# Seven block products in place of eight for two pairs of chunks of the second feed-forward

## The chip, the cores and the metric

The kernel runs on one core of a Trainium2 chip. A core has TensorE (PE; its weight loads are PEld), VectorE (DVE), ScalarE (ACT), GpSimd (POOL), SyncE (SP), whose queue issues most transfers, and 16 DMA engines. The on-chip memory SBUF has 128 partitions; matmul results go to banks of 128 x 512 fp32 in PSUM. The metric is the device time of one execution in microseconds. The median of three runs before is 800.43 us.

## What is computed

One residual block on x (256 tokens of 1024 values): a feed-forward, a mixer of two branches, a read of a memory by attention, and a second feed-forward. The change touches the last:

```python
def swiglu(h, w_in, w_down):
    gate, up = jnp.split(h @ w_in, 2, axis=-1)
    return (jax.nn.silu(gate) * up) @ w_down

h = rmsnorm(x, ffn2_pre_g[l])
x = x + 0.5 * rmsnorm(swiglu(h, ffn2_w_in[l], ffn2_w_down[l]), ffn2_post_g[l])
```

`w_in` is 1024 x 5632 (2816 gate and 2816 up columns), `w_down` 2816 x 1024.

## The kernel before

**Numbers.** Each fp32 operand of a large product is split into two fp32r parts, hi (a cast on ACT) and lo = operand − hi (a subtraction on DVE). A product is three matmuls: hi·hi, hi·lo, lo·hi. A weight "unit" is 128 x 1024 fp32, 512 KB: `load_split` (L118 to L128) loads it into one of 4 `raw` buffers over SP's queue, casts it into one of 8 `hi` buffers (L126) and subtracts into one of 8 `lo` buffers (L127). The same eight and eight serve all weights in turn.

**The feed-forward** (`ffn`). The inner width is cut into 11 chunks of 256 (NFF). A chunk's 512 columns (256 gate, 256 up) are four units; unit i holds the rows of two blocks kb = 2i and 2i + 1 of 128 each, side by side. `act_tok(c, h)` computes chunk c for token half h (128 tokens) in one PSUM bank (tag `mm`, two banks): 8 blocks x 3 = 24 matmuls of 128 x 128 by 128 x 512, the tokens transposed and stationary (`X.hi`, `X.lo`), the weights moving. `act_evac` applies silu on ACT (L354) and the product with the up half on DVE (L359); both scale by `r2[h]`, the per-token factor of the norm, so that TensorE works on unscaled tokens. `flush` transposes a finished chunk (four transposes, L349) and splits it into `acts`. `down(c, h)` is the second product: 2 units of `w_down`, 12 matmuls for each half, added up over all chunks in four banks of tag `acc`.

**Order.** In the second feed-forward chunks 0 and 1 run first for half 0, then for half 1 (the tokens of half 1 come later, from the block before). From chunk 2 on each step is `act_tok(c, 0)`, `act_tok(c, 1)`, `down(c − 2)` with a flush. The last three second products run at the end, half by half, with `post` and `post_last`. The framework places each instruction on its engine by readiness and program order; `after` ties a group behind a given matmul. Each engine takes its own instructions in the order that results, and a transfer waits in SP's queue until its buffer is free.

**Buffers.** Tag `m4` has 21 buffers of 4 KB in a partition, for tokens, activations, gain rows and whatever else is 128 x 1024. Tag `extra` has 4 of 4 KB: four of the eight `heads` loaded at the start (L460) and the four rows of gate biases (L829) use it. `row_of` (L244 to L253) turns the two per-token factors, one for each partition, into a row along the free axis on all partitions: two products of a diagonal matrix with ones, then a copy by ACT. GpSimd does next to nothing: some memsets, a few transfers, two selects, and one sum in `post_last` (L328) beside two DVE operations (L330).

Of the kernel before, what the change touches and what calls it, by code (L numbers as in the profile page):

```python
# [9 lines left out]
F32 = mybir.dt.float32  # L10
# [36 lines left out]
WARM = 8  # L47

X_AT = 11


_ORDER = [
# [15 lines left out]
def block_kernel(ctx: ExitStack, tc: tile.TileContext, wts, head_in, gf_in, x_in, mem_in, memT_in, cols, rows, fbias, masks, out):  # L68
# [12 lines left out]
    def MM(*args, **kw):  # L81
        log.append(PE.matmul(*args, **kw).ins)  # L82
# [9 lines left out]
    def nm(s):  # L92
        count[0] += 1
        return f"{s}_{count[0]}"

    def m4(shape, dt=F32, n="m"):
        return mp.tile(shape, dt, tag="m4", name=nm(n))
# [7 lines left out]
    def mm():  # L105
        return pp.tile([P, 512], F32, tag="mm", name=nm("mm"), bufs=2)

    def trp():
        return pp.tile([P, 512], F32, tag="tr", name=nm("tr"), bufs=2)
# [5 lines left out]
    def parts_of():  # L115
        return [wp.tile([P, D], F32R, tag=t, name=nm(t), bufs=8) for t in ("hi", "lo")]
# [27 lines left out]
    def split(hi, lo, src):  # L144
        S.copy(hi, src)  # L145
        V.tensor_tensor(out=lo, in0=src, in1=hi.bitcast(F32), op=ALU.subtract)
# [43 lines left out]
    def bc(a, shape, dim):  # L190
        return a.unsqueeze(dim).to_broadcast(shape)
# [52 lines left out]
    def row_of(r2):  # L244

        ps = trp()
        for h in range(2):
            dg = sp.tile([P, P], F32, tag="diag", name=nm("diag"), bufs=2)
            V.tensor_scalar(out=dg, in0=ident, scalar1=r2[h], scalar2=None, op0=ALU.mult)
            MM(ps[:, h * P : (h + 1) * P], ones, dg, start=True, stop=True)  # L250
        row = sp.tile([P, T], F32, tag="row", name=nm("row"), bufs=2)
        S.copy(row, ps[:, :T])
        return row  # L253

    def gain_split(X, kb, src, g, a=0, b=T, first=False):
# [4 lines left out]
            S.activation(X.hi(kb, a, b), src, AF.Copy, scale=gs)  # L260
        V.scalar_tensor_tensor(out=X.lo(kb, a, b), in0=src, scalar=gs, in1=X.hi(kb, a, b).bitcast(F32), op0=ALU.mult, op1=ALU.subtract)  # L261

    def to_T(X, src, h, g, qs=(0, 1)):

        for q in qs:
            ps = trp()
            for j in range(4):
                kb = 4 * q + j
                PE.transpose(ps[:, j * P : (j + 1) * P], src(kb), ident)  # L269
            for j in range(4):  # L270
                gain_split(X, 4 * q + j, ps[:, j * P : (j + 1) * P], g, h * P, h * P + P)
# [62 lines left out]
    def ffn(w_in, w_dn, X, r2, n_tok, i_row, first_half, second_half=None):  # L334

        acts = {}
        late = []
        ats = {}

        def flush(n):  # L340

            if late:
                c = late.pop(0)
                tr = trp()
                trv = tr.rearrange("p (j t) -> p j t", j=2)
                with after(n):
                    for h in range(2):
                        for j in range(2):
                            PE.transpose(trv[:, j, h * P : (h + 1) * P], ats[c, h][:, j * P : (j + 1) * P], ident)  # L349
                    split(acts[c][:, 0], acts[c][:, 1], trv)  # L350

        def act_evac(ps, c, h):
            sg = sp.tile([P, FC], F32, tag="c1", name=nm("sg"), bufs=7)
            silu = S.activation(sg, ps[:, :FC], AF.Silu, scale=r2[h])  # L354
            if c == NFF - 1 and h == 1 and not first_half:
                with tc.issue_after(silu.ins):
                    S.activation(warm, ones[:, 0:1], AF.Sqrt)
            a = sp.tile([P, FC], F32, tag="c1", name=nm("at"), bufs=7)
            V.scalar_tensor_tensor(out=a, in0=ps[:, FC:], scalar=r2[h], in1=sg, op0=ALU.mult, op1=ALU.mult)  # L359
            ats[c, h] = a  # L360
            if h == 1:
                late.append(c)

        def act_tok(c, h):
            ps = mm()
            proj_tok(ps, X, chunk(w_in, c), h)
            act_evac(ps, c, h)

        def act_first(c, bank):

            u = chunk(w_in, c)
            outs = [bank(), bank()]
            for kb in range(KB):
                wh, wl = blk(u, kb)
                for i in range(3):
                    for h in range(2):
                        a, b = h * P, h * P + P
                        x, w = ((X.hi(kb, a, b), wh), (X.lo(kb, a, b), wh), (X.hi(kb, a, b), wl))[i]
                        MM(outs[h], x, w, start=(kb == 0 and i == 0), stop=(kb == KB - 1 and i == 2))
            return outs  # L380

        def down(c, h, cols=((0, 512), (512, 1024))):
            act = acts[c]
            hs = slice(h * P, (h + 1) * P)
            for j in range(2):
                wh, wl = unit(w_dn, 2 * c + j)
                ah, al = act[:, 0, j, hs], act[:, 1, j, hs]
                for lo, up in cols:
                    for i, (a, w) in enumerate(((ah, wh), (ah, wl), (al, wh))):
                        MM(accs[h][lo // 512][:, lo % 512 : lo % 512 + up - lo], a, w[:, lo:up], start=(c == 0 and j == 0 and i == 0), stop=(c == NFF - 1 and j == 1 and i == 2))  # L390

        for c in range(n_tok):
            acts[c] = m4([P, 2, 2, T], F32R, "act")
        for h in range(2):
            m = len(log)
            for c in range(n_tok):
                act_tok(c, h)
            if h == 0 and n_tok:
                second_half(m)
        accs = None  # L400
        done = 0
        if callable(r2):
            outs = [act_first(c, acc) for c in range(2)]
            r2 = r2()
            for c in range(2):
                acts[c] = m4([P, 2, 2, T], F32R, "act")
                for h in range(2):
                    act_evac(outs[c][h], c, h)
            n_tok = 2
        for c in range(n_tok, NFF):  # L410
            acts[c] = m4([P, 2, 2, T], F32R, "act")
            if c == 2 and first_half:
                n = len(log)
                outs = act_first(c, mm)
                for h in range(2):
                    flush(n + L_ACT + 24 * h)
                    act_evac(outs[h], c, h)
            else:
                for h in range(2):
                    n = len(log)  # L420
                    act_tok(c, h)
                    if c == 2 or c > NFF - STAG + 1:
                        flush(n + L_ACT)
            if c == 6:
                grow = load_row(i_row)
                if first_half:
                    with tc.issue_after(loads[-1]):
                        nc.sync.dma_start(masks_s, masks)
            if accs is None:
                accs = [[acc(), acc()], [acc(), acc()]]  # L430
            while done < min(c - 1, NFF - STAG):
                n = len(log)
                for h in range(2):
                    down(done, h)
                flush(n + L_ACT)
                done += 1
        left, right = (0, 512), (512, 1024)
        m = len(log)
        for cut in (left, right):
            for c in range(NFF - STAG, NFF):  # L440
                down(c, 0, (cut,))
        flush(m + L_ACT)
        post(accs[0], 0, grow, 0.5, not first_half)
        m = len(log)
        if first_half:
            for c in range(NFF - STAG, NFF):
                down(c, 1)
            first_half(m)
            post(accs[1], 1, grow, 0.5)
        else:  # L450
            for cut in (left, right):
                for c in range(NFF - STAG, NFF):
                    down(c, 1, (cut,))
            post_last(accs[1], 1, grow, 0.5)
# [2 lines left out]


    X1 = Pair()
    heads = [wp.tile([P, D], F32, tag="raw" if kb < 4 else "extra", name=nm("head"), bufs=4) for kb in range(KB)]  # L460
    for kb in range(KB):
        loads.append(nc.sync.dma_start(heads[kb][:, : T + 512 + KB], head_in[kb]).ins)

# [358 lines left out]


    zs = []

    def gates(c):
        u = chunk("gates", c)
        z = m4([P, 2, 512], n="zg")
        brow = wp.tile([P, D], F32, tag="extra", name=nm("brow"), bufs=4)[:, :512]  # L829
        with tc.issue_after(loads[-1]):  # L830
            nc.sync.dma_start(brow, rows[4 + c // 2, c % 2 * 512 : c % 2 * 512 + 512].partition_broadcast(P))
        for h in range(2):
            ps = mm()
            proj_tok(ps, X2, u, h)
            V.scalar_tensor_tensor(out=z[:, h], in0=ps, scalar=r2[h], in1=brow, op0=ALU.mult, op1=ALU.add)
        zs.append(z)
# [268 lines left out]
```

## Time and profile before

| | us |
|---|---|
| median of three runs (lowest, highest) | 800.43 (800.04, 800.54) |
| span of the profiled execution, first to last instruction | 798.5 |
| mean granted TensorE clock in it | 0.999 |
| ACT busy in the span | 418.6 |
| second feed-forward from chunk 3 to the end of chunk 9 | 645.87 to 763.50 |
| span from 776.18 to the end (last second products and norm) | 22.32 |

The profile gives the profiled execution by its span; what lies before the first and after the last instruction is in the time of the runs only. In lines of groups the columns are line, engine, operation, out<-in with shapes, count, then busy us and the mean ns of one, then the idle time of the engine ahead of them and what ended it. In the chain of waits each line has its start, its length and the work. In windows each engine's busy time stands with the number of its instructions behind it; the last three numbers are the granted clock, the DMA share and GB/s.

### The profile page before, as it was taken

The numbers are of one execution on the slowest core, as the hardware profiler recorded it, in microseconds if no ns is written. First come the engines' busy times: TensorE is split into PE (matmuls) and PEld (weight loads), VectorE is DVE, ScalarE is ACT, GpSimd is POOL, SyncE is SP. The second block draws the span as 40 slices with busy tenths as digits, with TensorE's granted clock in tenths as the row PEclk, the third lists the DMA queues.
The fourth block names the chain that finished last, engine by engine and source line by source line (L and its number), as shares of the span: only waits on it lengthen the run. The fifth ranks groups of instructions, "written<-read, shape, count | busy, mean of one in ns | idle before, by whom it ended". The sixth has DMA issues, their size and how long they took to land.

```text
span 798.5 us, 12835 instructions
## 1 busy us (share of the span) xinstructions
PE 789.4 (99%) x5068; PEld 682.3 (85%) x5068; DVE 520.4 (65%) x824; ACT 418.6 (52%) x636; POOL 9.2 (1%) x21
## 2 busy tenths in 40 slices
PE   9999999999999999999999999999999999999996
PEld 7888888888899999998888888999888888888885
DVE  6765545548766898578675765965649754545543
ACT  7655345446853447348574445655647654434541
POOL 0000000000000100100000000000000000000000
PEclk9999999999999999999999999999999999999999
DMA  9775654664545555744476655556443666664521
GB/s 348 244 262 210 219 181 161 198 219 149 170 160 142 179 188 161 237 146 140 156 272 236 199 173 166 159 185 203 143 145 131 212 190 215 205 203 163 181 83 53
DMA packets 43692, 147.45 MB, mean 185 GB/s; under 512 B 4840, under 2 KB 8304, under 8 KB 43632
## 3 DMA queue, kind: packets, MB, share of 16 engines
q1 hardware_dynamic: 43024, 144.92, 54.7%
q0 software_dynamic: 464, 1.58, 0.7%
q8 instruction: 40, 0.66, 0.3%
q14 instruction: 20, 0.16, 0.1%
q10 hardware_dynamic: 144, 0.13, 0.0%
HBM read 145.56 MB, written 1.06 MB: 184 GB/s over the span
## 4 chain that ended last, share of the span: by engine, by line
PE 98%; DMA 0%; DVE 0%; issue 0%; ACT 0%; DVEq 0%; ACTq 0%
PE mm L82 67%; PE acc L82 27%; PE tr L349 1%; PE tr L82 1%; PE tr L269 1%; DMA head<-in_head_dram 0%; PE tr L785 0%; PE tr L871 0%; PE tr L974 0%; DVEq L1101 0%; DVE xs L330 0%; DVE post L315 0%; ACT hi L475 0%; ACT hT L145 0%; ACT junk L232 0%
## 5 line engine op out<-in xcount | busy, mean ns | idle before, releaser
L127 DVE TENSOR_TENSOR lo<-raw,hi 128x1024 fp32r<-128x1024 f32 (+1 forms) x260 | 311.3, 1206 | 124.7 <-ACT hi L126 115.7
L126 ACT CAST hi<-raw 128x1024 fp32r<-128x1024 f32 (+1 forms) x260 | 266.4, 1038 | 156.2 <-PE mm L82 95.2
L82 PE MATMUL mm<-hi,hT 128*128 128x512 f32 (+1 forms) x592 | 227.0, 386 | 0.0
L82 PE MATMUL mm<-lo,hT 128*128 128x512 f32 (+1 forms) x592 | 227.0, 386 | 0.0
L82 PE MATMUL mm<-hi,lT 128*128 128x512 f32 (+1 forms) x592 | 226.3, 386 | 0.0
L82 PEld LDWEIGHTS mm<-hi,hT 128*128 128x128 f32 x592 | 111.1, 188 | 21.9 <-ACT hT L260 0.5
L82 PEld LDWEIGHTS mm<-hi,lT 128*128 128x128 f32 x592 | 111.1, 188 | 21.8 <-DVE lT L261 0.5
L82 PEld LDWEIGHTS mm<-lo,hT 128*128 128x128 f32 x592 | 111.0, 188 | 20.6
L82 PE MATMUL acc<-hi,act 128*128 128x512 f32 x352 | 111.9, 390 | 0.0
L82 PE MATMUL mm<-hT,hi 128*128 128x256 f32 x384 | 109.0, 284 | 0.1
L82 PE MATMUL mm<-hT,lo 128*128 128x256 f32 x384 | 109.0, 284 | 0.0
L82 PE MATMUL mm<-lT,hi 128*128 128x256 f32 x384 | 108.9, 284 | 0.0
L82 PEld LDWEIGHTS acc<-hi,act 128*128 128x128 f32 x352 | 66.1, 188 | 13.2
L82 PEld LDWEIGHTS mm<-hT,hi 128*128 128x128 f32 x384 | 73.6, 192 | 0.4 <-issue 0.3
L82 PEld LDWEIGHTS mm<-hT,lo 128*128 128x128 f32 x384 | 73.6, 192 | 0.1
L82 PEld LDWEIGHTS mm<-lT,hi 128*128 128x128 f32 x384 | 73.6, 192 | 0.1
L82 PE MATMUL acc<-lo,act 128*128 128x512 f32 x176 | 70.0, 398 | 0.0
L354 ACT ACTIVATE sg<-mm,rstd 128x256 f32<-128x256 f32 x40 | 19.0, 475 | 75.0 <-PE mm L82 75.0
L359 DVE SCALAR_TENSOR_TENSOR at<-mm,rstd,sg 128x256 f32<-128x256 f32 x40 | 19.2, 481 | 57.1 <-ACT sg L354 57.1
L82 PEld LDWEIGHTS acc<-lo,act 128*128 128x128 f32 x176 | 33.1, 188 | 6.2
L82 PE MATMUL acc<-hi,hT 128*128 128x512 f32 x96 | 35.3, 395 | 0.2
L82 PE MATMUL acc<-hi,lT 128*128 128x512 f32 x96 | 35.3, 395 | 0.0
(194 smaller groups left out, 644.9 us busy)
## 6 DMA issues: line engine op xcount, KB each, us to landing
raw<-in_wts_dram SPq DMA_DIRECT2D x248, 512.0 KB, 4.5
raw<-in_gf_dram SPq DMA_DIRECT2D x12, 344.0 KB, 3.9
head<-in_head_dram SPq DMA_DIRECT2D x8, 388.0 KB, 6.1
grow<-in_rows_dram SPq DMA_DIRECT2D x4, 512.0 KB, 5.5
xs<-in_x_dram SPq DMA_DIRECT2D x2, 512.0 KB, 8.6
cbm<-cd POOLq DMA_DIRECT2D x2, 512.0 KB, 7.0
brow<-in_rows_dram SPq DMA_DIRECT2D x4, 256.0 KB, 5.5
memT<-in_memT_dram SPq DMA_DIRECT2D x2, 512.0 KB, 6.8
```

Source lines behind the costliest of these rows:

```text
L82: log.append(PE.matmul(*args, **kw).ins)
L126: S.copy(h, r)
L127: V.tensor_tensor(out=l, in0=r, in1=h.bitcast(F32), op=ALU.subtract)
L269: PE.transpose(ps[:, j * P : (j + 1) * P], src(kb), ident)
L349: PE.transpose(trv[:, j, h * P : (h + 1) * P], ats[c, h][:, j * P : (j + 1) * P], ident)
L354: silu = S.activation(sg, ps[:, :FC], AF.Silu, scale=r2[h])
L359: V.scalar_tensor_tensor(out=a, in0=ps[:, FC:], scalar=r2[h], in1=sg, op0=ALU.mult, op1=ALU.mult)
```

## The change

Chunks 4 and 5, and chunks 7 and 8, are computed together (a "quad", `QUADS = (4, 7)`). The tokens are cut in two halves h, the 1024 rows of the weights into even and odd blocks j, the columns into the two chunks. That makes a 2 x 2 by 2 x 2 product of blocks, each block product 4 row blocks x 3 = 12 matmuls. Winograd's form of Strassen's scheme computes it with 7 block products: X00·B11, X01·B21, S1·T1, S2·T2, S3·T3, X11·T4, S4·B22. S1 to S4 are sums of token blocks, T1 to T4 sums of weight blocks.

Since tokens of the two halves are now added, the per-token factor must be in them: `mixed`, called once after chunk 2, adds hi and lo of the tokens, multiplies by the row of factors, and splits again (GpSimd, then ACT and DVE); it forms and splits S1 to S4. From chunk 3 on all chunks use the scaled tokens, and `act_evac` has no scale.

In `quad` the units of the first chunk go to `raw`, those of the second to two buffers `wide` of two units each. GpSimd forms A = B11 + B12 and E = B21 + B22 unit by unit, then T2 = A + B22, T3 = B12 + B22 and T4 = A + E, in the order of the code; T1 is A. `two` splits each sum. B12 itself is never split, and B11, B21 and B22 are. Partial results are copied out of PSUM by ACT (`keep`) and combined on DVE. The second products `down(n_down, ...)` of the two chunks that are due stand between the block products, half by half. No flush stands inside a quad; chunk 6 and chunk 9 flush after each half instead.

`heads` 4 to 7 and the gate-bias rows use halves of `wide` in place of `extra`.

```diff
+QUADS = (4, 7)
+    def mixed(X, r):
+        row = row_of(r)
+        full = [m4([P, 4, T], n="full") for _ in range(2)]
+        for f, xh, xl in zip(full, X.h, X.l):
+            G.tensor_tensor(out=f, in0=xh.bitcast(F32), in1=xl.bitcast(F32), op=ALU.add)
+            G.tensor_tensor(out=f, in0=f, in1=bc(row, [P, 4, T], 1), op=ALU.mult)
+        N = Pair()
+        for q in range(2):
+            split(N.h[q], N.l[q], full[q])
+        sums = [m4([P, 2, 4, P], n="sums") for _ in range(2)]
+        s1_, s2_, s3_, s4_ = (t[:, i] for t in sums for i in range(2))
+        def form(o, x, y, op):
+            for q in range(2):
+                G.tensor_tensor(out=o[:, 2 * q : 2 * q + 2], in0=x(q), in1=y(q), op=op)
...
+        form(s1_, block(1, 0), block(1, 1), ALU.subtract)
+        form(s2_, of(s1_), block(0, 0), ALU.subtract)
+        form(s3_, block(0, 0), block(1, 0), ALU.subtract)
+        form(s4_, block(0, 1), of(s2_), ALU.add)
+        out = []
+        for t in sums:
+            hi, lo = m4([P, 2, 4, P], F32R, "sh"), m4([P, 2, 4, P], F32R, "sl")
+            split(hi, lo, t)
+            out += [(hi[:, i], lo[:, i]) for i in range(2)]
+        return N, out
...
         def act_evac(ps, c, h):
             sg = sp.tile([P, FC], F32, tag="c1", name=nm("sg"), bufs=7)
-            silu = S.activation(sg, ps[:, :FC], AF.Silu, scale=r2[h])
+            if mix:
+                silu = S.activation(sg, ps[:, :FC], AF.Silu)
+            else:
+                silu = S.activation(sg, ps[:, :FC], AF.Silu, scale=r2[h])
...
-            if h == 1:
+            if (c, 1 - h) in ats:
                 late.append(c)
+        def quad(c, n_down):
+            N, ((s1h, s1l), (s2h, s2l), (s3h, s3l), (s4h, s4l)) = mix[0]
+            for k in (c, c + 1):
+                acts[k] = m4([P, 2, 2, T], F32R, "act")
+            def two(src):
+                hi, lo = (p.rearrange("p (i n) -> p i n", i=2) for p in parts_of())
+                split(hi, lo, src)
+                return [(hi[:, i], lo[:, i]) for i in range(2)]
+            B11, B21, T1, wide, ones_, sums = [], [], [], [], [], []
+            for q in range(2):
+                W = wp.tile([P, 2, 2, 512], F32, tag="wide", name=nm("wide"), bufs=2)
+                A, E = m4([P, 2, 512], n="ta"), m4([P, 2, 512], n="te")
+                for i in range(2):
+                    u = _AT[w_in] + 4 * c + 2 * q + i
+                    raw = wp.tile([P, D], F32, tag="raw", name=nm("raw"), bufs=4)
+                    loads.append(nc.sync.dma_start(raw, wts[u - 4]).ins)
+                    loads.append(nc.sync.dma_start(W[:, i].rearrange("p j n -> p (j n)"), wts[u]).ins)
+                    hi, lo = parts_of()
+                    split(hi, lo, raw)
+                    B11.append((hi[:, :512], lo[:, :512]))
+                    B21.append((hi[:, 512:], lo[:, 512:]))
+                    G.tensor_tensor(out=A[:, i], in0=raw[:, :512], in1=W[:, i, 0], op=ALU.add)
+                    G.tensor_tensor(out=E[:, i], in0=raw[:, 512:], in1=W[:, i, 1], op=ALU.add)
+                wide.append(W)
+                ones_.append((A, E))
+            for A, E in ones_:
+                T1 += two(A)
...
+            b1, b2, b3 = mm(), mm(), trp()
+            for i in range(4):
+                prod(b1, X(0, 0), B11, i, True)
+                prod(b3, X(0, 1), B21, i, True, True)
+            p1 = keep(b1)
+            prods(b2, F(s1h, s1l), T1, True)
+            V.tensor_tensor(out=p1, in0=p1, in1=b3, op=ALU.add)
+            act_evac(p1, c, 0)
+            T2 = []
+            for (A, E), W in zip(ones_, wide):
+                t = m4([P, 2, 512], n="t2")
+                G.tensor_tensor(out=t, in0=A, in1=W[:, :, 1], op=ALU.add)
+                T2 += two(t)
+            down(n_down, 0)
+            prods(b1, F(s2h, s2l), T2, False)
+            w = keep(b1)
+            T3 = []
+            for W in wide:
+                t = m4([P, 2, 512], n="t3")
+                G.tensor_tensor(out=t, in0=W[:, :, 0], in1=W[:, :, 1], op=ALU.add)
+                T3 += two(t)
+            down(n_down, 1)
+            prods(b1, F(s3h, s3l), T3, False)
+            v = keep(b1)
+            V.tensor_tensor(out=v, in0=b2, in1=v, op=ALU.subtract)
+            act_evac(v, c + 1, 1)
+            T4 = []
+            for A, E in ones_:
+                G.tensor_tensor(out=E, in0=A, in1=E, op=ALU.add)
+                T4 += two(E)
+            down(n_down + 1, 0)
+            prods(b1, X(1, 1), T4, False, True)
+            act_evac(b1, c, 1)
+            B22 = []
+            for W in wide:
+                B22 += two(W[:, :, 1])
+            down(n_down + 1, 1)
+            prods(b2, F(s4h, s4l), B22, False, True)
+            V.tensor_tensor(out=w, in0=b2, in1=w, op=ALU.subtract)
+            act_evac(w, c + 1, 0)
...
+            if not first_half and c in QUADS:
+                quad(c, done)
+                done += 2
+                continue
...
-                    if c == 2 or c > NFF - STAG + 1:
+                    if c == 2 or c > NFF - STAG + 1 or c - 2 in QUADS and not first_half:
                         flush(n + L_ACT)
+            if c == QUADS[0] - 2 and not first_half:
+                mix.append(mixed(X, r2))
+                X = mix[0][0]
...
-    heads = [wp.tile([P, D], F32, tag="raw" if kb < 4 else "extra", name=nm("head"), bufs=4) for kb in range(KB)]
+    heads = [wp.tile([P, D], F32, tag="raw", name=nm("head"), bufs=4) for kb in range(4)]
+    for _ in range(2):
+        wide = wp.tile([P, 2, D], F32, tag="wide", name=nm("head"), bufs=2)
+        heads += [wide[:, 0], wide[:, 1]]
```

`prod` is three matmuls (hi·hi, hi·lo, lo·hi) of one row block, `prods` four of these, `X(h, j)` a block of the scaled tokens, `F` one of the token sums.

More of the change, by code (lines that the diff above doesn't have):

```diff
@@ L261, in gain_split, with of, block @@
         V.scalar_tensor_tensor(out=X.lo(kb, a, b), in0=src, scalar=gs, in1=X.hi(kb, a, b).bitcast(F32), op0=ALU.mult, op1=ALU.subtract)
+    def mixed(X, r):
[12 more added lines that the diff above has]
+                G.tensor_tensor(out=o[:, 2 * q : 2 * q + 2], in0=x(q), in1=y(q), op=op)
+        def of(t):
+            return lambda q: t[:, 2 * q : 2 * q + 2]
+        def block(h, j):
+            return lambda q: full[q][:, :, h * P : h * P + P].rearrange("p (k e) t -> p k e t", e=2)[:, :, j]
+        form(s1_, block(1, 0), block(1, 1), ALU.subtract)
[8 more added lines that the diff above has]
+        return N, out
     def to_T(X, src, h, g, qs=(0, 1)):
@@ L350, in flush @@
                     split(acts[c][:, 0], acts[c][:, 1], trv)
+        mix = []
         def act_evac(ps, c, h):
             sg = sp.tile([P, FC], F32, tag="c1", name=nm("sg"), bufs=7)
-            silu = S.activation(sg, ps[:, :FC], AF.Silu, scale=r2[h])
+            if mix:
+                silu = S.activation(sg, ps[:, :FC], AF.Silu)
+            else:
+                silu = S.activation(sg, ps[:, :FC], AF.Silu, scale=r2[h])
             if c == NFF - 1 and h == 1 and not first_half:
@@ L358, in act_evac, with X, F, prod @@
             a = sp.tile([P, FC], F32, tag="c1", name=nm("at"), bufs=7)
-            V.scalar_tensor_tensor(out=a, in0=ps[:, FC:], scalar=r2[h], in1=sg, op0=ALU.mult, op1=ALU.mult)
+            if mix:
+                V.tensor_tensor(out=a, in0=ps[:, FC:], in1=sg, op=ALU.mult)
+            else:
+                V.scalar_tensor_tensor(out=a, in0=ps[:, FC:], scalar=r2[h], in1=sg, op0=ALU.mult, op1=ALU.mult)
             ats[c, h] = a
-            if h == 1:
+            if (c, 1 - h) in ats:
                 late.append(c)
+        def quad(c, n_down):
[25 more added lines that the diff above has]
+                T1 += two(A)
+            def X(h, j):
+                hs = slice(h * P, h * P + P)
+                return lambda i: (N.hi(2 * i + j)[:, hs], N.lo(2 * i + j)[:, hs])
+            def F(h, l):
+                return lambda i: (h[:, i], l[:, i])
+            def prod(ps, A, B, i, start, stop=False):
+                (ah, al), (bh, bl) = A(i), B[i]
+                MM(ps, ah, bh, start=start and i == 0, stop=False, skip_group_check=True)
+                MM(ps, ah, bl, start=False, stop=False, skip_group_check=True)
+                MM(ps, al, bh, start=False, stop=i == 3, skip_group_check=True)
+            def prods(ps, A, B, start, stop=False):
+                for i in range(4):
+                    prod(ps, A, B, i, start, stop)
+            def keep(ps):
+                t = sp.tile([P, 512], F32, tag="z2", name=nm("keep"), bufs=3)
+                S.copy(t, ps)
+                return t
+            b1, b2, b3 = mm(), mm(), trp()
+            for i in range(4):
+                prod(b1, X(0, 0), B11, i, True)
[36 more added lines that the diff above has]
+            act_evac(w, c + 1, 0)
@@ L410, in ffn @@
         for c in range(n_tok, NFF):
+            if c in acts:
+                continue
+            if not first_half and c in QUADS:
+                quad(c, done)
+                done += 2
+                continue
             acts[c] = m4([P, 2, 2, T], F32R, "act")
@@ L824, in block_kernel @@
     zs = []
+    brows = []
     def gates(c):
@@ L828, in gates @@
         z = m4([P, 2, 512], n="zg")
-        brow = wp.tile([P, D], F32, tag="extra", name=nm("brow"), bufs=4)[:, :512]
+        if c % 2 == 0:
+            brows.append(wp.tile([P, 2, D], F32, tag="wide", name=nm("brow"), bufs=2))
+        brow = brows[-1][:, c % 2, :512]
         with tc.issue_after(loads[-1]):
```

## The prediction

> **What bounds the kernel now.** The page comes first: the span, the busy shares, the chain of work that ended last.
>
> ```profile
> span 798.5 us, 12835 instructions
> PE 789.4 (99%) x5068; PEld 682.3 (85%) x5068; DVE 520.4 (65%) x824; ACT 418.6 (52%) x636; POOL 9.2 (1%) x21
> PE 98%; DMA 0%; DVE 0%; issue 0%; ACT 0%; DVEq 0%; ACTq 0%
> ```
>
> TensorE alone sets the time, and GpSimd (POOL) stands still: fewer matmuls shorten the kernel exactly as long as nothing else falls behind. Next the chain in order of time (start, length, work), in the stretch that the change rebuilds.
>
> ```profile
> 639.93 5.03 PE acc L82 x22
> 644.96 0.44 PE tr L349 x4
> 645.40 0.47 PE acc L82 x2
> 645.87 10.91 PE mm L82 x48
> 656.78 4.99 PE acc L82 x22
> 661.77 0.44 PE tr L349 x4
> 662.20 0.46 PE acc L82 x2
> 662.66 10.92 PE mm L82 x48
> ```
>
> One chunk of the second feed-forward is 48 first products (10.91 us, 0.2273 us each), 24 second products and four transposes. Chunk 2 ends its first products at 639.93, chunk 3 runs 645.87 to 662.66, chunk 4 begins at 662.66. Then the windows by chunk (length, then busy us of PE, PEld, DVE, ACT, POOL) and the helpers' groups there:
>
> ```profile
> 645.87:662.66 16.79, 16.79 (x77) 13.89 (x77) 8.82 (x10) 7.63 (x10) 0.00 (x0) 1.00 0.59 187
> 662.66:679.48 16.82, 16.82 (x78) 13.91 (x77) 8.85 (x10) 7.65 (x10) 0.00 (x0) 1.00 0.57 191
> ```
> ```profile
> L127 DVE TENSOR_TENSOR lo<-raw,hi 128x1024 fp32r<-128x1024 f32 x55 | 67.4, 1225 | 37.8 <-ACT hi L126 35.0
> L126 ACT CAST hi<-raw 128x1024 fp32r<-128x1024 f32 x54 | 56.8, 1052 | 36.9 <-PE acc L82 21.3 <-PE mm L82 13.1 <-DMA raw<-in_wts_dram 2.5
> ```
>
> A chunk takes 16.8 us; DVE works 8.8 us of it, nearly all in six "lo" subtractions. Those have two inputs, raw and hi, both in SBUF. That matters below.
>
> **What it removes.** Two chunks cost 8 block products of 12 matmuls, a quad 7: 12 matmuls, 2.73 us, and over two quads 5.45 us. It adds `row_of`:
>
> ```profile
> L82 PE MATMUL tr<-diag,ones 128*128 128x128 f32 x8 | 1.2, 274 | 0.0
> L252 ACT COPY row<-tr x2: 362/362/363, 216.3 to 488.5; 128x256 f32<-128x256 f32 x2
> ```
>
> Two calls made those 8 matmuls in 1.2 us: 0.6 us on TensorE, then 0.36 us for the copy. Net on TensorE: −4.85 us.
>
> **What it adds beside TensorE.** A split is one cast on ACT and one lo on DVE. A quad has 14 of 1024 elements in place of 8 (four for B11 and B21, two each for T1, T2, T3, T4 and B22); with the four second-product units that is 18. ACT then has 18 × 1.05 us, three copies of a PSUM bank and four Silu, and DVE 18 lo, three bank sums and four products.
>
> ```profile
> L651 ACT COPY aux<-acc 128x512 f32<-128x512 f32 x2 | 1.2, 587 | 0.7 <-PE acc L82 0.7
> L887 DVE TENSOR_TENSOR zg<-mm,zg 128x512 f32<-128x512 f32 x8 | 5.5, 688 | 8.5 <-PE mm L82 8.5
> L359 DVE SCALAR_TENSOR_TENSOR at<-mm,rstd,sg 128x256 f32<-128x256 f32 x20 | 9.6, 480 | 30.4 <-ACT sg L354 30.4
> ```
>
> ACT: 18.9 + 3 × 0.59 + 4 × 0.48 (a Silu taken like the product) = 22.6 us; DVE: 18 × 1.225 + 3 × 0.69 + 4 × 0.48 = 26.0 us. The quad's 84 + 48 matmuls last 30.0 us, so each engine alone is covered, DVE barely. The loads are the same bytes. The renamed buffers for heads and gate biases change owner, not number: nothing.
>
> GpSimd gets the rest. In elements per partition: scaled tokens 2 sums and 2 multiplications of 1024; token sums 8 × 256; in a quad 8 × 512 for A and E and 6 × 1024 for T2, T3, T4, which is 10,240. No such row of 1024 exists; the nearest are these.
>
> ```profile
> 793.56 1.61 DVE L330 SCALAR_TENSOR_TENSOR xs<-post,y,xs 128x512 f32<-128x512 f32 x2
> 794.15 0.74 POOL L328 TENSOR_TENSOR xs<-post,xs 128x256 f32<-128x256 f32 x1 [462.45 <-ACT post L327]
> ```
> ```profile
> L739 POOL TENSOR_SCALAR_AFFINE_SELECT cbm<-cbm 128x1024 f32<-128x1024 f32 x2 | 2.2, 1088 | 6.4 <-DMA cbm<-cd 6.4
> L630 POOL MEMSET f<- 64x512 f32 x2 | 1.0, 523 | 102.8 <-DVE k L622 102.8
> L581 POOL MEMSET aux<- 128x256 f32 x2 | 0.6, 312 | 169.4 <-PE acc L82 161.7 <-PE mm L82 7.7
> ```
> ```profile
> L330 DVE SCALAR_TENSOR_TENSOR xs<-post,y,xs 128x256 f32<-128x256 f32 x1 | 0.9, 946 | 0.0
> L330 DVE SCALAR_TENSOR_TENSOR xs<-post,y,xs 128x512 f32<-128x512 f32 x1 | 0.8, 753 | 0.0
> ```
>
> The two memsets give a fixed part of 0.10 us (523 − 312 is 0.21 for 256 elements). The one two-input operation then costs (0.741 − 0.10) / 256 = 2.5 ns an element, or 2.2 if it first waited the 0.07 us until DVE's first operation was through (794.22, below). I take 2.4. Bounds: 2.9 if nothing is fixed (0.741 / 256), 1.06 by the one-input select (1.088 / 1024).
>
> The Trainium skill, GPSIMD Engine Reference, § 3.1 gives 4497 ns for 2048 elements; taken as 2.2 ns an element, the sum below would end, as an estimate, at 811 in place of 816 us.
>
> **The shared path.** The last fence holds the decisive row. DVE's 256-element operation took 946 ns, its 512-element neighbour 753. It began at 793.56 + 1.61 − 0.946 = 794.22, 0.07 us after GpSimd's; GpSimd ended at 794.89, DVE at 795.17. That is DVE standing until GpSimd is done and then needing 0.28 us for 256 elements. So a DVE operation with two SBUF inputs and a GpSimd operation go one after the other, not side by side. Whether GpSimd waits for DVE likewise, no row shows; the sum needs only that their times add.
>
> The Trainium skill, SBUF — State Buffer, § Who interferes with whom, has the rule for both directions: DVE's second SBUF input comes through the read interface of GpSimd, and the later one blocks. Were it only a slowdown of both by part, the sum would lie between 795.6 and 816 us; the row agrees with the block.
>
> ```profile
> 305.04 1.19 DVE L127 TENSOR_TENSOR lo<-raw,hi 128x1024 fp32r<-128x1024 f32 x1
> 306.15 0.74 DVE L699 SCALAR_TENSOR_TENSOR k_b<-mm,row 128x256 f32<-128x256 f32 x2
> ```
>
> A lo inside a queue costs its pitch: the next operation starts 306.15 − 305.04 = 1.11 us later; I use 1.12 (0.28 × 4).
>
> **First quad.** The chain runs from the row to T4, the last operand from GpSimd. Row: 639.93 + 0.6 + 0.36 = 640.9. The sums of hi and lo ahead of the multiplications need no row and are done by then. From 640.9 GpSimd owes 2048 + 2048 + 10,240 elements: 34.4 us. DVE's lo from 641.4 to 663.85, by its groups in that window before:
>
> ```profile
> L127 DVE TENSOR_TENSOR lo<-raw,hi 128x1024 fp32r<-128x1024 f32 x9 | 11.0, 1226 | 6.8 <-ACT hi L126 6.5
> ```
>
> These nine stay (by the order of need three of chunk 3, two of second product 1 and four of chunk 4, now B11 and B21). New are two for the scaled tokens, two for the token sums, two each for T1 to T4; two for second product 2 go between. 23 × 1.12 = 25.8 us. Together 60.2 us. TensorE wants T4's last part late: chunk 3 begins at 645.87 + 0.6, quad one 16.79 us later at 663.3, then 96 matmuls (21.8 us) and six of T4's own (1.4): 686.5, or 45.6 us after the row. TensorE waits 60.2 − 45.6 = **14.6 us**, in pieces ahead of T1, T2, T3 and T4. Queued behind the late sums are the casts and lo of the second-product units and, on SP's queue, the loads into raw buffers that GpSimd hasn't read; all wait for the same stretch, so they are in the sum.
>
> ```profile
> raw<-in_wts_dram SPq DMA_DIRECT2D x248, 512.0 KB, 4.5
> ```
>
> **Second quad.** From T4 of the first to T4 of the second TensorE has 36 matmuls, chunk 6 (72, with three sets of transposes, 1.3 us) and 96: 47.7 us. GpSimd can't start at once: the two wide weight tiles are free only after B22 is split, four lo or 4.5 us later, and the load lands 4.5 us after that (above). In those 9 us DVE does six lo of 24 (two of the second product, two B22, two of chunk 6); 18 are left, 20.2 us; GpSimd's 10,240 elements are 24.6. 9 + 20.2 + 24.6 − 47.7 = **6.1 us**. The last chunks have DVE's old load and hide what lags.
>
> **Sum.** Span 798.5 − 5.45 + 0.6 + 14.6 + 6.1 = 814.4 us. The median of the runs, 800.43, lies 1.9 us above this span; the same about the new one gives 816 us. With 2.9 ns an element the waits are 21.8 and 11.2: 829 us. With 1.06 both are nothing: 795.6.
>
> **Rivals.**
> First, the two engines do not exclude each other over whole operations: lo and sums run side by side. GpSimd alone owes 34.4 us and 24 × 0.10 fixed from 640.9, ends at 677.7, and T4 is split by 679.9 (1.05 + 1.12 later), before 685.1 when TensorE starts on it. Then the net on TensorE stands: 795.6 us, faster. It decides from where 38% of DVE's 25.8 us pass under GpSimd (34.4 + 16.0 − 45.6 = 4.85, the gain). For it: only one row speaks for exclusion. Against it: that row fits to 0.01 us (256 elements in 0.28 are DVE's plain pitch).
>
> ```profile
> L261 DVE SCALAR_TENSOR_TENSOR lT<-tr,cols_s,hT x8: 343/348/353, 616.3 to 621.1; 128x128 fp32r<-128x128 f32 x8
> ```
>
> Second, the scaled tokens come later still: GpSimd takes sum, multiplication, sum, multiplication in program order behind the row, so that 2048 more elements, 4.9 us, lie on the first quad's chain, and chunk 3 waits as well: 821 us. Against it: the first sums need only the tokens, whose last lT starts at 621.1 us (above).
> Third, exclusion holds but GpSimd is quicker, near 1.8 ns an element: 25.8 + 25.8 − 45.6 is 6.0, and 9 + 20.2 + 18.4 − 47.7 is nothing: 801.6 us, no change to speak of.
> That fewer matmuls aren't issued isn't open: they're counted.
>
> **How the numbers follow.** The forecast, 816 us (its own range 807 to 829), has 0.60; the late tokens 0.10; side by side 0.25; the draw 0.05. A measurement of this kernel tells about 0.2%, 1.6 us. So faster 0.25, same 0.05, slower 0.70. The range goes from 795 us, which takes in the first rival, to 829 us, the upper price of GpSimd.
>
> **What would show it.** Right: some 65 to 100 us busy on POOL; lo inside the quads well over 1.225 us, where they meet GpSimd; TensorE idle ahead of products with T1 to T4, named as waiting for hi or lo, and those for GpSimd's sums; the first quad longer than the second. Wrong: lo at 1.2 us under running sums (first rival); idle time ahead of chunk 3 (second); a GpSimd sum of 1024 under 1.9 us (third). The 21 shared data tiles are all taken in the second quad (scaled tokens 4, token sums 4, gain row 1, activations 4, A and E 4, T2 and T3 4): a wait for one is in no term.

## The result, and the profile after

The changed kernel takes 825.36 us (median of 4 runs), the kernel before on the same chip 800.48: a ratio of 1.0304, interval 1.0289 to 1.0319, slower by 24.9 us. The profiled execution of the changed kernel spans 821.2 us against 798.5; it is the fastest of the four (823.06 us), so that its account ends 2.2 us short of the 24.9. The prediction had 816 us, range 795 to 829, and 0.70 for slower.

The page of the changed kernel: span, busy shares, chain of work.

```profile
span 821.2 us, 12898 instructions
PE 792.4 (96%) x5048; PEld 682.2 (83%) x5048; DVE 568.7 (69%) x848; ACT 435.6 (53%) x659; POOL 94.3 (11%) x61
PE 90%; POOL 3%; DVE 3%; issue 3%; ACT 1%; DVEq 0%; POOLq 0%; ACTq 0%
```

The chain that was 98% TensorE now runs through GpSimd, DVE and what lies between them for 9%. POOL's 94.3 us are at the upper end of the 65 to 100 us that the prediction set as its sign. TensorE's waits from 610 us on in the changed kernel (who waited for whom: total, times, longest):

```profile
PE acc L84 <- DVE lo L129: 9.2, 3, 4.8
PE acc L84 <- ACT hi L128: 5.1, 1, 5.1
PE mm L84 <- DVE lo L148: 1.7, 2, 1.2
PE mm L84 <- DVE at L403: 1.6, 1, 1.6
PE mm L84 <- DVE lT L148: 1.6, 1, 1.6
```

L128 and L129 are the cast and the lo of weights that need no sum; L148 is the lo of `split`, which also serves the sums. The long waits are for the former, weights of the second product (`acc`), and not for T1 to T4. Why, the chain shows in the first quad (start, length, work):

```profile
673.07 3.33 POOL t L472
676.43 1.05 ACT hi L147
...
680.38 0.73 DVE lo L148
681.11 1.91 issue
683.02 2.57 DVE at L401
685.59 6.61 DVE lo L129 x2
692.20 0.04 issue
692.24 2.50 PE acc L84 x5
694.74 1.99 PE mm L84 x7
696.74 2.72 PE acc L84 x12
```

A product `at` of 256 elements takes 2.57 us, and two lo take 6.61, where one took 1.225 before. They stand in DVE's queue behind T2 and under GpSimd's sums; TensorE waits for them. Behind the wait 12 matmuls take 4.49 us instead of 2.72.

Only operations with two inputs in SBUF stand like that. L401 makes its product from a PSUM bank (`mm`) or from a copy in SBUF (`keep`); its instructions from 640 to 760 us (min, median, max in ns):

```profile
L401 DVE TENSOR_TENSOR at<-mm,sg x5: 407/411/417, 662.0 to 726.1; 128x256 f32<-128x256 f32 x5
L401 DVE TENSOR_TENSOR at<-keep,sg x4: 410/968/2569, 683.0 to 744.9; 128x256 f32<-128x256 f32 x4
```

Four of the five from PSUM began under a running GpSimd sum (the one at 661.99, for example, under the sum of 660.34 to 662.63), and none took longer than 0.417 us. GpSimd's own timeline, four rows of the changed kernel, of one or two sums:

```profile
659.09 1.30 POOL L432 TENSOR_TENSOR ta<-raw,wide 128x512 f32<-128x512 f32 x1
660.34 2.29 POOL L433 TENSOR_TENSOR te<-raw,wide 128x512 f32<-128x512 f32 x1
...
678.66 6.65 POOL L480 TENSOR_TENSOR t<-wide 128x1024 f32<-128x1024 f32 x2
...
726.73 4.74 POOL L472 TENSOR_TENSOR t<-ta,wide 128x1024 f32<-128x1024 f32 x2
```

A sum of 512 elements takes 1.30 or 2.29 us, a sum of 1024 2.37 or 3.33. Of the 32 sums of these two sizes 28 lie within 0.05 us of one of these values: a sum either runs freely or stands for one whole lo, 1.0 us. Four lie between (1.44, 1.47, 2.53 and 3.10 us). The one of 3.10 began at 643.22, when a lo of 1.23 us had been running since 642.83, and stood for the rest of it. So GpSimd waits for DVE just as DVE for GpSimd, which the one row of before could not show. Two free sizes give 2.1 ns an element, (2.37 − 1.30) / 512, and about 0.2 us fixed; 2.46 and 1.23 us were taken for the two sizes. The Trainium skill, SBUF — State Buffer, § Who interferes with whom, states this block in both directions for DVE instructions with two SBUF inputs; the trace agrees, at 1.0 us for each lo met.

The windows of the first quad in the changed kernel (length, busy us by engine, granted clock, DMA share, GB/s):

```profile
674.00:680.00 6.00, 1.64 (x7) 0.86 (x5) 2.65 (x3) 2.80 (x4) 6.00 (x3) 0.86 0.26 87
680.00:686.00 6.00, 3.35 (x7) 2.15 (x7) 6.00 (x4) 3.69 (x5) 6.00 (x3) 0.50 0.00 0
686.00:692.30 6.30, 2.56 (x6) 1.55 (x6) 6.30 (x3) 2.47 (x3) 5.10 (x2) 0.50 0.28 83
692.30:697.00 4.70, 4.70 (x14) 3.76 (x15) 4.70 (x5) 1.28 (x2) 0.00 (x0) 0.67 0.36 115
```

DVE and GpSimd are both "busy" without a gap from 680 to 686, and only four and three instructions fall into these 6 us: DVE's busy time here is mostly standing. After a wait of 5.14 us TensorE's clock is granted at 0.50, and it is still low when the operands have come, until about 696.7. The Trainium skill, TensorE: Matmul & The Clock Gate, Part 1, says that an idle window of some 3.4 us halves the clock; the trace agrees.

From the chain's starts the stages compare like this; "due" is the stage before less the matmuls saved, plus 0.6 us for the row, with the transposes where they now stand (0.44 us a set). The quads end 12 × 0.2267 us behind 710.34 and 765.82, where the chain has their last products.

| stage | before | due | after | lost |
|---|---|---|---|---|
| chunks 0 and 1 of half 1, chunk 2 | 616.32 to 639.93: 23.61 | 23.6 | 615.79 to 641.34: 25.55 | 1.9 |
| to the end of the first quad | 639.93 to 696.28: 56.35 | 53.3 | 641.34 to 713.06: 71.72 | 18.4 |
| chunk 6 and the second quad | 696.28 to 746.71: 50.43 | 47.7 | 713.06 to 768.54: 55.48 | 7.8 |

Lost 28.1, saved 4.85; the first stage began 0.5 us earlier than before, and that leaves the 22.7 us between the spans.

### The profile page after: what moved, and what is told of

Its sections match the earlier page's. It is cut to its first block, busy times and chain, and to the rows that moved or that the text cites. A ratio compares the mean times of both kernels' runs of the same rounds, so it can differ in the third digit from the quotient of the medians.

```text
span 821.2 us, 12898 instructions
## 1 busy us (share of the span) xinstructions
PE 792.4 (96%) x5048; PEld 682.2 (83%) x5048; DVE 568.7 (69%) x848; ACT 435.6 (53%) x659; POOL 94.3 (11%) x61
## 4 chain that ended last, share of the span: by engine, by line
PE 90%; POOL 3%; DVE 3%; issue 3%; ACT 1%; DVEq 0%; POOLq 0%; ACTq 0%
PE mm L84 60%; PE acc L84 25%; PE tr L84 1%; POOL sums L280 1%; DVE lo L148 1%; PE tr L385 1%; DVE lo L129 1%; PE tr L305 1%; POOL ta L432 1%; POOL te L433 1%; POOL t L472 0%; DVE at L401 0%; PE tr L935 0%; POOL full L271 0%; ACT hi L147 0%
## 5 line engine op out<-in xcount | busy, mean ns | idle before, releaser
L129 DVE TENSOR_TENSOR lo<-raw,hi 128x1024 fp32r<-128x1024 f32 (+1 forms) x244 | 299.2, 1238 | 102.1 <-ACT hi L128 95.1
L128 ACT CAST hi<-raw 128x1024 fp32r<-128x1024 f32 (+1 forms) x244 | 249.2, 1036 | 144.6 <-PE mm L84 92.4
L84 PE MATMUL mm<-hi,hT 128*128 128x512 f32 (+1 forms) x544 | 208.5, 386 | 1.7 <-DVE at L403 1.6
L84 PE MATMUL mm<-hi,lT 128*128 128x512 f32 (+1 forms) x544 | 207.7, 385 | 1.6 <-DVE lT L148 1.6
L84 PE MATMUL mm<-lo,hT 128*128 128x512 f32 (+1 forms) x544 | 208.8, 386 | 0.0
L84 PEld LDWEIGHTS mm<-hi,hT 128*128 128x128 f32 x544 | 102.2, 188 | 22.1 <-DVE at L403 2.1
L84 PEld LDWEIGHTS mm<-hi,lT 128*128 128x128 f32 x544 | 102.1, 188 | 21.7 <-DVE lT L148 2.0
L84 PEld LDWEIGHTS mm<-lo,hT 128*128 128x128 f32 x544 | 102.1, 188 | 18.5
L270 POOL TENSOR_TENSOR full<-hT,lT 128x1024 f32<-128x1024 f32 x2 | 5.7, 2890 | 289.6 <-DVE lT L263 289.6
L84 PE MATMUL acc<-hi,lT 128*128 128x512 f32 x96 | 35.2, 393 | 0.0
L84 PE MATMUL acc<-lo,hT 128*128 128x512 f32 x96 | 34.9, 391 | 0.0
```

The costliest lines, as they stand in the source:

```text
L128: S.copy(h, r)
L129: V.tensor_tensor(out=l, in0=r, in1=h.bitcast(F32), op=ALU.subtract)
L270: G.tensor_tensor(out=f, in0=xh.bitcast(F32), in1=xl.bitcast(F32), op=ALU.add)
```

## The experiments

Theory S (shared path): a DVE operation with two SBUF inputs and a GpSimd sum never run at once, so their times add. Rivals: the extra splits alone fill ACT and DVE; TensorE waits for the results of a slow GpSimd; the order in DVE's queue is at fault; the token work costs nothing. Ratios are against the kernel before on the same chip, 800.7 to 800.9 us each time.

**Without sums of weights.** `A`, `E`, `t2`, `t3` and the sum of T4 go; for example

```diff
-                G.tensor_tensor(out=t, in0=W[:, :, 0], in1=W[:, :, 1], op=ALU.add)
-                T3 += two(t)
+                T3 += two(W[:, :, 0])
```

> Leaves out A, E and the sums of T2, T3 and T4: GpSimd only scales the tokens and forms S1 to S4; T1 to T4 are split straight from the wide weight tiles, so the output is not the block's. All 14 splits of a quad, all matmuls and all loads stay. Shared path (DVE's two-input operations and GpSimd's sums go one after the other): TensorE no longer waits in the quads; 800.4 - 4.85 and 1.9 to 3.5 us for the early token sums that stay: 797.5 to 799 us. Rival, the six extra splits of a quad are too much for ACT and DVE by themselves: still over 812 us.

Measured 800.3 us, 0.9992 (0.9983 to 1.0001). The 25 us are gone, so 14 splits a quad fit on ACT and DVE: the first rival falls. But the gain isn't there either, and the value is 1.3 us above S's range. The chain of this run has the last products of each quad with the first of the next chunk in one piece:

```profile
694.94 7.71 PE mm L84 x34
...
742.64 7.71 PE mm L84 x34
```

From one to the other, chunk 6 and the second quad, are the 47.7 us due; the loss lies ahead.

**The same sums, read by nobody.** GpSimd makes as many sums of the same sizes, A and E from the wide tiles alone; the splits read the wide tiles.

```diff
-                T2 += two(t)
+                T2 += two(W[:, :, 1])
```

> As the run without weight sums, but GpSimd makes the same sums, same number and sizes, from the wide tiles into tiles that no split reads (T1 to T4 are again split straight from the wide tiles; the output is not the block's). Shared path: nobody waits for a sum's result, yet each lo under the sums waits for one; up to T4 23 lo alternate with up to 26 sums, so 808 to 825 us. Rival, the waits are for the results of a slow GpSimd only: 797.5 to 799 us, as without sums.

Measured 819.71 us, 1.0237 (1.0216 to 1.0257): 19.4 us above the run without sums, though no instruction needs a sum's result, and no wait of another engine in this run is named for a weight sum. This is the test between S and "slow results", and it speaks for S. TensorE's waits in this run:

```profile
PE acc L84 <- DVE lo L129: 10.7, 3, 6.9
PE tr L385 <- DVE at L401: 2.9, 1, 2.9
```

The remaining 825.4 − 819.7 = 5.7 us of the change belong to waiting for results and to queue order together.

**All sums on DVE.** Every `G.tensor_tensor` in `mixed` and `quad` becomes `V.tensor_tensor`.

> Every sum of the change runs on DVE in place of GpSimd; result as the reference. Shared path: DVE's 1024-element sum costs its pitch, 1.12 us, against 2.37 us and more on GpSimd with DVE standing. From the row to T4 the sums are 16.5 us, the lo 25.8, the rest of DVE about 5: 47 us in 45.6, so some 2 us of waiting: 796.5 to 801 us. Rival, DVE is too full in a quad whoever makes the sums: over 815 us.

Measured 805.58 us, 1.0056 (1.0041 to 1.0071): 20 us better than on GpSimd, though DVE now does all the work; 4.6 us worse than S's range allowed. Two windows of this run, the first quad and the second:

```profile
665.00:699.00 34.00, 31.23 (x128) 24.68 (x127) 33.36 (x36) 20.66 (x24) 0.00 (x0) 0.95 0.52 163
716.70:751.40 34.70, 31.59 (x134) 24.40 (x133) 34.14 (x37) 21.14 (x26) 0.00 (x0) 1.00 0.44 140
```

DVE is busy for 33.4 of 34.0 and 34.1 of 34.7 us, against 30.0 us of matmuls. The estimate spread DVE's work over chunk 3 and the quad; most of it can only run inside the quad.

**Second-product weights first.** In the quad the two units of the first second product are loaded and split ahead of T1.

```diff
+            for j in range(2):
+                unit(w_dn, 2 * n_down + j)
             for A, E in ones_:
                 T1 += two(A)
```

> The weights of the first second product in a quad are loaded and split ahead of T1 in place of behind T2; the rest as changed. TensorE's longest waits in the first quad are named for these splits. Shared path: the sum of DVE's and GpSimd's work up to T4 is the same, so the wait only moves ahead of T1 or T2: 821 to 828 us. Rival, the order in DVE's and ACT's queues is the cause (operands that need no sum queued behind ones that do): 811 to 818 us.

Measured 821.17 us, 1.0248 (1.0231 to 1.0265), 4.2 us better than the change. TensorE's waits of this run:

```profile
PE mm L84 <- DVE lo L148: 8.7, 6, 2.9
PE acc L84 <- DVE lo L129: 2.7, 2, 1.6
```

The wait has moved from `acc` to the products with sums (L148). Queue order is worth some 4 us of 25; S's range, at its lower edge, holds.

**Tokens only.** `QUADS = ()`, and `mixed` is called after chunk 2.

> No quad at all: only the tokens are scaled and S1 to S4 formed on GpSimd after chunk 2, and every chunk from 3 on uses the scaled tokens; result as the reference. In the run without weight sums TensorE waits 1.6 us before the end of chunk 2 and 1.6 us in chunk 3, and the row costs 0.6 us: 803.5 to 805.5 us. Rival, the scaled tokens cost nothing and the run without weight sums missed its gain inside the quads: 800.5 to 801.5 us.

Measured 805.38 us, 1.0057 (1.0042 to 1.0072): 4.7 us for the scaled tokens and their sums alone. The two waits of 1.6 us in the list above are theirs: GpSimd's first sums start as soon as the tokens are there, at 620.80 in the changed kernel, and hold up three lo and the product `at` behind them (L403), which frees the PSUM bank that TensorE wants next; the second wait is for the scaled tokens' own lo, in chunk 3.

**Neither.** No sums of weights, and `mixed` on DVE: GpSimd does nothing of the change.

> No sum of weights (T1 to T4 split straight from the wide tiles, output not the block's), and the scaling of tokens and S1 to S4 on DVE: GpSimd does nothing of the change. Shared path and the count of matmuls: 800.4 - 4.85 and at most 0.5 for DVE's token sums: 795.3 to 797 us. Rival, the 14 splits of a quad or the form of the quad cost TensorE by themselves: 799 us or more.

Measured 794.9 us, 0.9927 (0.9910 to 0.9943): −5.8 us, 0.4 us below S's range. The matmuls that the scheme saves are real, and with no weight sums, and the token sums on DVE, no wait of TensorE is left in the profile from 600 us to 790.

**Sums added to the kernel before.** Three or six sums a chunk from chunk 3 on, of data that is finished, into tiles that nobody reads:

```diff
+                if not first_half and done > 1:
+                    for _ in range(6):
+                        u = acts[done].rearrange("p a j t -> p (a j t)").bitcast(F32)
+                        v = m4([P, D], n="extra")
+                        G.tensor_tensor(out=v, in0=u, in1=u, op=ALU.add)
```

> The kernel before, and in each chunk from 3 on GpSimd makes 3 sums of 1024 elements of finished activations, which nothing reads. Shared path: 3 x 2.37 + 6 x 1.12 = 13.8 us of a chunk's 16.8: no change, 800 to 802 us. Rival, any work of GpSimd delays DVE's lo on TensorE's path: 803 us or more.

> The same with 6 unread sums in each of 7 chunks. Shared path: 6 x 2.37 + 6 x 1.12 = 20.9 us in a chunk of 16.8: 4.1 us or more a chunk, less what runs ahead: 820 to 840 us. Rival, the two engines slow each other only in part, or not: under 810 us.

With three, 801.49 us, 1.0006 (0.9997 to 1.0016): no change. With six, 806.98 us, 1.0076 (1.0061 to 1.0091): far under S's range and inside the rival's. Read by groups, the sums of this run (min, median, max in ns):

```profile
L441 POOL TENSOR_TENSOR extra<-act x42: 1884/2837/2892, 647.7 to 767.9; 128x1024 f32<-128x1024 f32 x42
```

A sum of a tile with itself is free at 1.88 us, not 2.37, and 2.84 us when it met a lo. Six sums at 1.88 and six lo at 1.0 are 17.3 us, little more than the chunk's 16.8. So the price was wrong, or the theory. To tell these apart, the same with `in1=X.h[0]`, a second tile:

> The kernel before with 6 unread GpSimd sums a chunk as in the run before this, but with two different tiles as inputs, as the sums of weights have. With one tile read twice a sum held 1.85 us, and 1.0 us more when it met a lo; the chunk took 17.9 us. Shared path: 2.3 + 1.0 us for a pair of sum and lo, six pairs 19.8 us in place of 16.8: 3 to 3.6 us in each of six or seven chunks, 818 to 826 us. Rival, exclusion is only part of it and the pitch of 17.9 us has another cause: 805 to 809 us, as with one tile.

Measured 819.26 us, 1.0235 (1.0216 to 1.0254), inside S's range. Groups and timeline of this run's sums:

```profile
L441 POOL TENSOR_TENSOR extra<-act,hT x42: 2387/3378/3403, 647.1 to 785.6; 128x1024 f32<-128x1024 f32 x42
```
```profile
688.91 100.05 POOL L441 TENSOR_TENSOR extra<-act,hT 128x1024 f32<-128x1024 f32 x30 [1.77 <-DVE act L146]
```

Thirty sums follow each other at 3.34 us: 2.34 for the sum, 1.0 for one lo in between. From 690 to 780 us DVE is busy for 88.93 of 90.0 us, a lo there takes 3.15 us on the mean instead of 1.225, and TensorE's waits (14.7 us from 640 us on) are all for products `at`, which stand behind lo in DVE's queue; none is for a buffer or a sum. In a kernel with no quad, with no result that anyone needs, this costs 18.5 us. The exclusion is measured by itself.

**Tokens on DVE, weight sums on GpSimd.**

> The changed kernel with the scaling of the tokens and S1 to S4 on DVE; the sums of weights stay on GpSimd; result as the reference. Shared path: the two waits of 1.6 us outside the quads go, and up to the first quad GpSimd has 9.8 us of sums less, DVE some 5 more, so the first quad's wait shrinks by up to 5 us: 816 to 821 us. Rival, the first quad waits for its weight sums alone and the token work is hidden there: 821.5 to 823.5 us.

Measured 824.46 us, 1.0296 (1.0278 to 1.0313): above both ranges. Three rows of this run, two of DVE's timeline and one of GpSimd's:

```profile
641.29 2.35 POOL L432 TENSOR_TENSOR ta<-raw,wide 128x512 f32<-128x512 f32 x1 [308.60 <-ACT hi L128]
```
```profile
657.95 4.04 DVE L280 TENSOR_TENSOR sums<-full 128x256 f32<-128x256 f32 x2
...
665.46 0.75 DVE L280 TENSOR_TENSOR sums<-full,sums 128x256 f32<-128x256 f32 x2
```

Freed of the tokens, GpSimd starts on A at 641.29 instead of 659.09, and now its weight sums collide with the token work: two DVE sums of 256 elements take 4.04 us under GpSimd's sums and 0.75 us without. TensorE's longest waits are now for transposes of activations, ahead of the first quad, and no shorter in sum:

```profile
PE tr L385 <- DVE at L401: 11.0, 2, 7.8
PE acc L84 <- DVE lo L129: 3.6, 1, 3.6
PE mm L84 <- DVE lT L148: 3.5, 1, 3.5
```

**One quad, all sums on DVE.** `QUADS = (7,)`, tokens after chunk 2.

> Only chunks 7 and 8 form a quad; the tokens are scaled after chunk 2 and every sum runs on DVE; result as the reference. TensorE saves 2.73 us and pays 0.6 for the row and up to 0.5 for the tokens; DVE has chunks 3 to 6 for the token sums and no earlier quad holds the wide tiles, so the second quad's wait of about 4.7 us (all sums on DVE, two quads) shrinks to 0 to 3 us: 798.5 to 802 us. Rival, DVE is full within a quad whatever lies ahead: 803 us or more.

Measured 803.05 us, 1.0028 (1.0018 to 1.0038), the rival's side by a hair, less than its runs spread (802.39 to 803.99). By its timeline seven of the eight adds for A and E start late, in order behind an activation's lo, and from that lo on DVE has no gap through the quad's sums:

```profile
714.04 0.69 DVE L148 TENSOR_TENSOR act<-tr,act 128x512 fp32r<-128x512 f32 x1 [4.60 <-ACT act L147]
```

DVE is idle for 4.60 us ahead of it. Whether another order would bring this version under the kernel before was not tried. No version here that makes the sums beats it.

## Why the prediction was right

**Gain on TensorE: right.** −4.85 us net was forecast; with nothing of the change on GpSimd and no sums of weights it is −5.8 (794.9 against 800.7). In the profiles 0.5 us of it lies ahead of the change: this run begins the first stage at 615.83, the kernel before at 616.32.

**Exclusion: right, from one row.** Sums that nobody reads cost 19.4 us in the changed kernel and 18.5 in the kernel before. The first rival (side by side, 0.25) falls with both. The third (GpSimd at 1.8 ns an element) falls with the 2.1 measured.

**GpSimd's and DVE's prices: near.** 2.37 and 1.30 us for sums taken as 2.46 and 1.23; a lo holds the path for 1.0 us, not 1.12. With the rates measured the sum up to T4 is about 58 us rather than 60.2: two multiplications of 1024 4.7, eight sums of 256 5.9 (0.2 and 256 × 2.1 ns each), eight of 512 10.4, six of 1024 14.2, and 23 lo 23.0. But only 18 lo lie between the row (there at 643.08) and the end of T4's last lo (694.38 + 2.35 = 696.73): those of chunk 3 and of second product 1 had begun before the row was there, the last of them at 642.83. The sums, 35.2 us, and 18 lo are 53.2 us; the trace has 53.65. So the times add, and the count of lo was too high.

**First quad: mechanism right, 14.6 us against 18.4.** The step that missed the place is "in pieces ahead of T1, T2, T3 and T4". TensorE stopped at the second product between them, whose cast and lo needed no sum but stood behind T2's in the queues; from there on the later sums were in time. T4's last part was ready at 696.73, 4.4 us ahead of the 701.1 that the prediction's sum gives (640.9 + 60.2), and TensorE came to T4 at 704.90: T4, whose readiness the sum prices, was not what TensorE waited for. That 14.6 came so near 18.4 is in part luck. The prediction named this queue and held it "in the sum"; putting those splits first gave back 4.2 us. A second part was left out: the halved clock after the long wait, 12 matmuls in 4.49 instead of 2.72 us, 1.8 us.

**Second quad: 6.1 against 7.8 us.** Shorter than the first, as forecast. Here too the nearness is in part luck. GpSimd began 15.7 us behind T4's last lo (712.45), not 9, and waited for a load into `raw`; from there to the end of the second T4's last lo (749.73 + 2.35 = 752.08) it took 39.6 us, not 44.8 (20.2 + 24.6). The clock step is in this quad as well, with a granted clock of 0.63 from 746.40 to 751.00; the first ten matmuls behind its wait, in the chain of the changed kernel:

```profile
744.85 0.41 DVE at L401
745.26 1.15 DVE lo L129
746.41 0.04 issue
746.46 4.14 PE acc L84 x10
```

4.14 us in place of 2.27 are 1.9 us, about the difference. (The product `at` ahead of it, with GpSimd through, takes 0.41 us.)

**Tokens: wrongly set at nothing.** "The sums of hi and lo ahead of the multiplications need no row and are done by then" is true, and they cost 1.9 us all the same: running early, they held up lo on TensorE's path. The second rival (they come late) didn't happen: both sums of hi and lo began some 20 us ahead of the row, at 620.80 and 623.17. Alone the token work costs 4.7 us.

Put together by differences of medians: −5.8 for the matmuls, +5.4 for the tokens on GpSimd (800.3 − 794.9), +19.4 for unread sums, +5.7 for results and order: 24.7 of the measured 24.9. Each run differs from the next by one of these, so they add up by the way they are formed; that is no test of its own. How the 5.7 divide isn't settled: order alone gave 4.2, but the two interact. Nor is it shown by experiment how much the clock costs; the figures above are read from the trace.

## What to carry to other kernels

Work given to an idle engine isn't free if that engine shares a path with a busy one: add the two engines' times in the stage, not the shares of the span. Here a DVE operation with two SBUF inputs can pay a whole GpSimd sum, whatever its own size, and all that stands behind it in DVE's queue pays with it, such as the products that release PSUM; on DVE itself the same sums cost 20 us less. And when a queue holds operands that need a late result and operands that need none, the ones without need go first: that was worth 4.2 us here.

## What the runs showed of the hardware

Exclusion comes by whole instructions: 14 of 16 sums of 1024 elements took about 2.37 us or about 3.35, and a 256-element product of two SBUF inputs on DVE between 0.41 us, free, and 2.57. A product of the same size with one input in PSUM took 0.41 us under running sums too. A GpSimd sum of a tile with itself is cheaper than one of two tiles: 1.88 against 2.39 us at 1024 elements, so that the test with one tile could not tell the theory from its rival.
